# A chunked recurrence on one core: three loads with stacked keys, second copies of the decays by transfer, memory parts handed back one by one

## The chip, the cores and the metric

One core of a Trainium2 chip. The metric is the device time of one execution in microseconds, the median of several runs. Engines are TensorE (PE, its weight loads PEld), VectorE (DVE), ScalarE (ACT), GpSimd (POOL) and SyncE (SP, which here only issues transfers).

## What is computed

One decoder layer, float32, 2048 tokens by 1024 features: RWKV-7 time mixing, a layer norm, a gated MLP with a causal convolution, a layer norm. The change lies in the recurrence of the time mixing, 16 heads of 64:

```
def step(state, inp):
    r_t, w_t, k_t, v_t, kk_t, a_t = inp
    sa = jnp.einsum('bhij,bhj->bhi', state, -kk_t)
    state = (state * w_t[:, :, None, :]
             + sa[..., None] * (kk_t * a_t)[:, :, None, :]
             + v_t[..., None] * k_t[:, :, None, :])
    return state, jnp.einsum('bhij,bhj->bhi', state, r_t)
```

## The kernel before, in words

The work falls into four stages. `a_nodes` computes the projections r, k, v and the decay, and stores them to DRAM. `s_nodes` (L758) runs the recurrence. `w_nodes` (L1188) normalises, gates and multiplies by the output matrix. `f_nodes` (L1448) is the MLP. Products in the projections and the MLP are made of three passes over a high and a low part of each operand.

No order is written by hand. Every piece of work is a node of a planner (`Plan`, L59) with an engine, an estimated duration, a priority, dependencies, and slots that it takes and gives back. `order` (L81) simulates the engines with these durations, starts at each free engine the ready node of lowest priority number whose slots are free, and emits the instructions in that order. Each engine, and SP with its transfers, then runs its queue in order. So a duration in the planner changes only the order.

The recurrence is turned into matrix form over chunks of 64 rows. 2048 rows are 16 tiles of 128 rows, two chunks c each. A tile is prepared in two halves h of 512 columns (8 heads, or 4 pairs p of heads e = 0, 1):

- one load brings five inputs r, kp, kkn, b, th of a half into one single-buffered tile l (L846 to L848, slot lds);
- csI is the running sum of th, a product with a triangular matrix (L850);
- three exponentials make the decays P, Pe and Pi (L855 to L863);
- r is multiplied by P (L879), kkn by Pe (L875), and both are transposed (L902) into AR (L905);
- b and kp are multiplied by Pi into BKn (L922 to L930): eight products of 64 rows by 256 columns, since b and v, or k and state, swap their row halves between the two heads of a pair. The last of them gives the slot lds back;
- BKn is transposed (L932) and copied into BKT, one tile per head with the other head's rows zero (L939 to L943; the zeros are set once, L811);
- G = BKT x AR, four 128-row products per chunk and head (L948), masked into Gm (L954).

After both halves of a tile the 32x32 diagonal blocks are inverted on VectorE in 31 dependent steps of a multiply and an add (L984 to L998). The blocks go there through DRAM: NU is stored (L965), read back as NUs (L972), the start value XU is copied from a constant (L977); the result goes back by XD (L1000) and XT (L1010), and is completed by two small products per chunk (L1020 to L1053). Then the state is carried over the two chunks (L1076 to L1159): copy the state into UV (L1107), Z, copy, SA, copy into UV, dS, add, multiply by PC; Y is the output. The v rows of UV come from DRAM in four transfers of 256-byte pieces (L1067). From tile 12 on the eight pairs of a chunk go in two groups.

AR, BKn, Gm and PC exist four times each. The first product of a tile takes one of each (L844, L880), the last Y product gives all four back (L1156).

Of the kernel before, what the change touches and what calls it, by code (L numbers as in the profile page):

```python
# [11 lines left out]
F32 = mybir.dt.float32  # L12
# [3 lines left out]
OP = mybir.AluOpType  # L16
# [120 lines left out]
class K:  # L137
# [43 lines left out]
    def run(self, phases="ASWF", scratch=None):  # L181
        tc, nc, a = self.tc, self.nc, self.a
        with ExitStack() as ctx:
# [3 lines left out]
            for t in range(NT):  # L187
# [3 lines left out]
                for h in range(2):  # L191
# [3 lines left out]
                    for i, q in enumerate(("r", "kp", "kkn", "b", "th")):  # L195
                        self.S[q, t, h] = s[0:128, i] if q == "kkn" else s[1:129, i]
                    self.S["kk0", t, h] = s[128:129, 2]
# [33 lines left out]
    def a_nodes(self, ctx, pl):  # L231
# [56 lines left out]
        for sw, (q, wi, mm, ml) in enumerate((("k", 1, 2, 4), ("r", 0, 0, 1), ("v", 2, 3, 5))):  # L288
# [271 lines left out]
            for nq, (g, h, tl) in enumerate(order):  # L560
# [194 lines left out]
              slots=dict(lds=1, pw=4, P=1, Pi=1, Pe=1, AR=4, BKn=4, Gm=4, PC=4, BKT=1, NUs=2, XU=2, XT0=1, XT1=1, X11=2, mp=1,  # L755
                         FT=2, UV=2, c0=1, c1=1, Y=1, Yt=1))

    def s_nodes(self, ctx, pl, n_1, n_2, w, f):  # L758
# [12 lines left out]
        st_bkt = [0]  # L771
        eo = lambda tl: tl.rearrange("q (p e) i -> q p e i", e=2)
        ends, end1, xds, stores = [], [], [], []
        def f_open1():

            nonlocal inv, wkp, ldp, pw, xui, triI, gmask, cols, gm4, nbI, nbIn, nbE, scE
# [7 lines left out]
            ldp = E(name="s_ld", bufs=sl["lds"])  # L784
            pw = E(name="s_pw", bufs=sl["pw"], space=PSUM)
            xui = inv.tile([128, 512], F32, name="c_xui", bufs=1)
# [4 lines left out]

            for i in range(sl["BKT"]):
                BKTs.append([wkp.tile([128, 4, 128], F32, name=f"BKT{i}{e}") for e in range(2)])
# [26 lines left out]
        def f_c():  # L820
            for x, nm in ((triI, "c_triI"), (cols, "c_cols"), (gmask, "c_gmask"), (xui, "c_xui")):
                self.ld(x, a[nm])
        inv = wkp = ldp = pw = xui = triI = gmask = cols = gm4 = nbI = nbIn = nbE = scE = None
        cst = wk = ch2 = sm = pm = pc = None
        chs, XTs, BKTs, SV, ZS, SW, V = [None] * sl["AR"], [], [], {}, {}, {}, {}
        n_o1 = pl.add("-", 0, 0, f_open1, [n_1])
        n_o2 = pl.add("-", 0, 0, f_open2, [n_o1, n_2])
        n_z1 = pl.add("POOL", 2.0, -9.0, f_zero1, [n_o1], lat=0.2)
# [8 lines left out]
        for t in range(NT):  # L837
# [3 lines left out]
            grams, pcs, ars = [], [], {}  # L841
            for h in range(2):
                hb = b + h * o["hs"]
                first = ("AR", "BKn", "Gm", "PC") if h == 0 else ()  # L844

                def f_load(t=t, h=h):  # L846
                    self.ld(tile_of(t, f"l{h}", ldp, [128, 5, 512], tag="lds"), self.S["in", t, h])
                n_l = pl.add("SP", 0.5, -9.0 if t + h == 0 else hb + o["lds"], f_load, [n_o1], take=("lds",), lat=5.2)  # L848

                def f_cs(t=t, h=h, tri=None, nm=None):  # L850
                    ps = tile_of(t, (nm, h), pw, [128, 512], tag="pw")
                    MM(ps, tri, V[t][f"l{h}"][:, 4])
                n_ci = pl.add("PE", 0.86, hb, lambda f=f_cs: f(tri=triI, nm="csI"), [n_l] + [n_c] * (t == 0), take=("pw",))

                def f_exp(t=t, h=h, nm=None, src=None, bias=None, sc=None):  # L855
                    x = tile_of(t, (nm, h), wkp, [128, 512], tag=nm, bufs=sl[nm])
                    nc.scalar.activation(x, V[t][src, h], AF.Exp, bias=bias, scale=sc)
                n_P = pl.add("ACT", 0.57, hb + 0.2, lambda f=f_exp: f(nm="P", src="csI", bias=nbI, sc=-CDEC),
                             [n_ci], take=("P",))
                n_Pe = pl.add("ACT", 0.57, hb + 0.3, lambda f=f_exp: f(nm="Pe", src="csI", bias=nbE, sc=scE),  # L860
                              [n_ci, n_P], take=("Pe",))
                n_Pi = pl.add("ACT", 0.57, hb + 0.4, lambda f=f_exp: f(nm="Pi", src="csI", bias=nbIn, sc=CDEC),
                              [n_ci, n_Pe], take=("Pi",), give=("pw",))  # L863

                def f_alloc(t=t):
                    tile_of(t, "AR", chs[t % len(chs)], [128, 2, 8, 2, 64])
                    tile_of(t, "BKn", chs[t % len(chs)], [128, 2, 16, 64])
                    tile_of(t, "Gm", chs[t % len(chs)], [128, 2, 2, 8, 128])
                    tile_of(t, "PC", inv, [128, 8, 2], bufs=sl["PC"])

                def f_M(t=t, h=h, first=h == 0, f_alloc=f_alloc):
                    l = V[t][f"l{h}"]
                    if first:
                        f_alloc()
                    TT(l[:, 2], l[:, 2], V[t]["Pe", h], op=OP.mult)  # L875

                def f_R(t=t, h=h):
                    l = V[t][f"l{h}"]
                    TT(l[:, 0], l[:, 0], V[t]["P", h], op=OP.mult)  # L879
                n_M = pl.add("DVE", 0.6, hb + 0.5, f_M, [n_Pe] + [n_o2] * (t > 0 and h == 0), take=first, give=("Pe",))  # L880
                if h == 0:
                    n_alloc = n_M
                n_R = pl.add("DVE", 0.6, hb + 0.6, f_R, [n_P])

                def f_pcp(t=t, h=h):
                    pcp = tile_of(t, ("pcp", h), pw, [128, 4, 2, 64], tag="pw")
                    for p in range(4):
                        nc.tensor.transpose(pcp[:, p].rearrange("q c t -> q (c t)"),
                                            V[t]["P", h][:, p * 128:(p + 1) * 128], self.ident)
# [916 lines left out]
```

## Time and profile before

| | us |
|---|---|
| median of 3 runs (lowest to highest) | 2947.77 (2944.63 to 2948.37) |
| the profiled execution, its own time | 2945.05 |
| its span, first to last instruction | 2943.1 |
| busy in the span: TensorE / VectorE / ScalarE | 2803.2 / 2086.2 / 1742.4 |

A busy share is an average over four stages with different limits; the stages have to be looked at one by one. Matmuls overlap in their records, so the time of one record is longer than its share of the engine.

### The profile page before, as it was taken

Reading aid. Unit: us, or ns where it says so; the run is one execution under the profiler, and the core shown is the slowest. Engines: PE = TensorE matmul, PEld = TensorE weight load, DVE = VectorE, ACT = ScalarE, POOL = GpSimd, SP = SyncE. Lnnn points to the kernel's source line nnn. Section 1 sums busy time; section 2 is a strip of 40 time slices with the busy share of each in tenths; the row PEclk is TensorE's granted clock in tenths of the full one; section 3 lists DMA queues with packets and bytes.
Section 4 is the critical chain, followed back from the end, with each engine's and each line's share of the span. In section 5 each row is a group of like instructions: output and inputs, shape, how many; then the busy total and the mean of one; then the engine's idle time right before and its main releaser. Section 6 shows DMA issues by size and latency. Waiting matters only on the chain.

```text
span 2943.1 us, 51765 instructions
## 1 busy us (share of the span) xinstructions
PE 2803.2 (95%) x19392; PEld 2317.1 (79%) x19392; DVE 2086.2 (71%) x4288; ACT 1742.4 (59%) x4668; POOL 53.7 (2%) x96
## 2 busy tenths in 40 slices
PE   7998999998789999789999999999999999999997
PEld 5776778887677777678888888888888888888886
DVE  7888768986899999779865555475554745548454
ACT  8888657764578877887554444444444444444441
POOL 0000000001000000001100000000000000000000
PEclk9999999999899999899999999999999999999999
DMA  6446555435456656568652323343333432334222
GB/s 199 148 167 220 184 186 185 158 119 176 120 151 160 161 159 157 140 207 307 208 185 95 101 96 121 98 151 101 101 119 99 153 98 90 129 97 159 92 90 79
DMA packets 298555, 424.08 MB, mean 144 GB/s; under 512 B 153952, under 2 KB 179552, under 8 KB 294208
## 3 DMA queue, kind: packets, MB, share of 16 engines
q1 hardware_dynamic: 286976, 379.87, 41.3%
q0 software_dynamic: 11328, 40.90, 3.9%
q8 instruction: 153, 2.51, 0.4%
q14 instruction: 98, 0.80, 0.1%
HBM read 311.57 MB, written 109.12 MB: 143 GB/s over the span
## 4 chain that ended last, share of the span: by engine, by line
issue 55%; PE 21%; DVE 12%; ACT 7%; DMA 3%; POOL 1%; SPq 0%; POOLq 0%; ACTq 0%; DVEq 0%
PE ps L164 4%; PE ps L165 4%; PE ps L166 4%; DVE BKn L928 3%; ACT junk L643 2%; PE G L768 2%; DVE XU L995 2%; DVE itmp L990 2%; DVE Gm L955 1%; DMA l<-in 1%; PE Y L768 1%; DMA in<-av 1%; DVE l L879 1%; ACT junk L1283 1%; DVE l L875 1%
## 5 line engine op out<-in xcount | busy, mean ns | idle before, releaser
L166 PE MATMUL ps<-xH,wiL 128*128 128x512 f32 x1408 | 548.2, 389 | 0.5 <-DVE wiL L1594 0.5
L164 PE MATMUL ps<-xH,wiH 128*128 128x512 f32 x1408 | 548.1, 389 | 0.0
L165 PE MATMUL ps<-xL,wiH 128*128 128x512 f32 x1408 | 547.8, 389 | 0.0
L1594 DVE TENSOR_TENSOR wiL<-wis,wiH 128x1024 fp32r<-128x1024 f32 x176 | 215.4, 1224 | 459.0 <-ACT wiH L1455 459.0
L1455 ACT ACTIVATE hb<-ps 128x512 f32<-128x512 f32 x176 | 105.7, 601 | 484.4 <-PE ps L166 484.4
L164 PE MATMUL ps<-WH,xiH 128*128 128x512 f32 x768 | 305.1, 397 | 16.4 <-ACT xiH L255 9.5
L166 PEld LDWEIGHTS ps<-xH,wiL 128*128 128x128 f32 x1408 | 264.3, 188 | 56.9 <-DVE wiL L1594 2.1
L165 PEld LDWEIGHTS ps<-xL,wiH 128*128 128x128 f32 x1408 | 264.3, 188 | 54.8
L164 PEld LDWEIGHTS ps<-xH,wiH 128*128 128x128 f32 x1408 | 264.3, 188 | 54.6
L165 PE MATMUL ps<-WL,xiH 128*128 128x512 f32 x768 | 302.8, 394 | 2.2 <-DVE WL L350 2.2
L166 PE MATMUL ps<-WH,xiL 128*128 128x512 f32 x768 | 301.9, 393 | 0.0
L1622 DVE SCALAR_TENSOR_TENSOR cv<-hb,cw,cv 128x512 f32<-128x512 f32 x352 | 263.7, 749 | 19.9 <-ACT cv L1618 13.7
L165 PE MATMUL acc<-woL,aH 128*128 128x512 f32 x688 | 268.2, 390 | 2.2 <-DVE woL L1559 2.2
L164 PE MATMUL acc<-woH,aH 128*128 128x512 f32 x688 | 267.8, 389 | 0.0
L166 PE MATMUL acc<-woH,aL 128*128 128x512 f32 x688 | 267.7, 389 | 0.0
L1455 ACT ACTIVATE wiH<-wis 128x1024 fp32r<-128x1024 f32 x178 | 189.0, 1062 | 6.5 <-DMA wis<-in_w_in_dram 6.5
L164 PEld LDWEIGHTS ps<-WH,xiH 128*128 128x128 f32 x768 | 146.4, 191 | 54.6 <-ACT xiH L255 9.5
L1455 ACT ACTIVATE woH<-wos 128x512 fp32r<-128x512 f32 x172 | 108.7, 633 | 110.5 <-PE acc L166 103.9
L165 PEld LDWEIGHTS ps<-WL,xiH 128*128 128x128 f32 x768 | 146.3, 190 | 33.0 <-DVE WL L350 3.0
L166 PEld LDWEIGHTS ps<-WH,xiL 128*128 128x128 f32 x768 | 146.2, 190 | 31.2 <-DVE xiL L474 0.2
L165 PEld LDWEIGHTS acc<-woL,aH 128*128 128x128 f32 x688 | 129.1, 188 | 30.6 <-DVE woL L1559 4.0
L164 PEld LDWEIGHTS acc<-woH,aH 128*128 128x128 f32 x688 | 129.1, 188 | 27.4 <-ACT woH L1455 0.5
(243 smaller groups left out, 5349.3 us busy)
## 6 DMA issues: line engine op xcount, KB each, us to landing
wis<-in_w_in_dram SPq DMA_DIRECT2D x176, 512.0 KB
wos<-in_w_out_dram SPq DMA_DIRECT2D x172, 256.0 KB
l<-in SPq DMA_DIRECT2D x32, 1280.0 KB
xT<-in_xT_dram SPq DMA_DIRECT2D x21, 1028.0 KB
in<-kp SPq DMA_DIRECT2D x64, 256.0 KB
stg<-in_w_rkv_dram SPq DMA_DIRECT2D x48, 256.0 KB
gs<-gs SPq DMA_DIRECT2D x24, 512.0 KB
in<-kr SPq DMA_DIRECT2D x32, 256.0 KB
```

What stands on the lines that cost most here:

```text
L164: nc.tensor.matmul(ps, lH, rH, start=start, stop=False)
L165: nc.tensor.matmul(ps, lH, rL, start=False, stop=False)
L166: nc.tensor.matmul(ps, lL, rH, start=False, stop=stop)
L643: nc.scalar.activation(junk, Z["kr"][:, 64 * i:64 * i + 64], AF.Square, accum_out=st["ss"][:, tl, i:i + 1])
L768: MM = lambda out, l, r, **kw: nc.tensor.matmul(out, l, r, **{**dict(start=True, stop=True), **kw}, skip_group_check=True)
L875: TT(l[:, 2], l[:, 2], V[t]["Pe", h], op=OP.mult)
L928: TT(dst[rows, :, e], pe8(l[:, 1 if part else 3], e), pe8(V[t]["Pi", h], e), op=OP.mult)
L990: TT(V[t]["tv"], V[t]["XU"][:, 0:m, s:s + 1].to_broadcast([128, m, n]), V[t]["NUs"][:, s:s + 1, s + 1:32].to_broadcast([128, m, n]), op=OP ...
L995: TT(x, x, V[t]["tv"], op=OP.add)
L1455: CP = lambda out, in_, **kw: nc.scalar.activation(out, in_, AF.Copy, **kw)
L1594: TT(W["L"], W["s"], W["H"], op=OP.subtract)
L1622: STT(R[j], W["hb"][:, i:i + 512], C["cw"][:, fc, i:i + 1], R[j], op0=OP.mult, op1=OP.add)
```

## The change

The diff below is cut; "..." marks what is left out. In words:

- the five inputs are stored in the order r, kkn, b, kp, th and come in as three tiles with a slot each: th (lth), r and kkn (lrk), and b over kp stacked by chunk (lbk, two transfers): rows 0 to 63 of chunk c hold b, rows 64 to 127 hold kp, for all heads alike;
- P and Pe are two halves of one tile, and r and kkn are multiplied by them in one product of 128x1024;
- Pi is made by two exponentials of 64 rows, each on the rows of its chunk; two transfers inside SBUF then copy it to the other 64 rows, and one product of 128x1024 makes BKn;
- BKT is one 128-row tile with no zeros (two buffers), copied in one instruction; G uses rows 0 to 63 for head 0 and 64 to 127 for head 1, both heads in one node;
- all readers of the left blocks of Gm and of UV use rows 0 to 63 for both heads; the v rows of UV come in two transfers of whole rows; XU is loaded by SP and not copied by ScalarE;
- AR, Gm, BKn and PC are each taken where first written and given back where last read;
- many planner durations are changed, in the recurrence, the output projection and the MLP.

```
-                    for i, q in enumerate(("r", "kp", "kkn", "b", "th")):
+                    for i, q in enumerate(("r", "kkn", "b", "kp", "th")):
...
-              slots=dict(lds=1, pw=4, P=1, Pi=1, Pe=1, AR=4, BKn=4, Gm=4, PC=4, BKT=1, ...
+              slots=dict(cs=1, lth=1, lrk=1, lbk=1, pw=4, P=1, Pi=1, AR=4, BKn=4, Gm=4, PC=4, BKT=2, ...
...
-        def f_zero1():
-            for x in BKTs:
-                for e in range(2):
-                    nc.gpsimd.memset(x[e], 0.0)
...
-                n_l = pl.add("SP", 0.5, -9.0 if t + h == 0 else hb + o["lds"], f_load, [n_o1], take=("lds",), lat=5.2)
+                def f_lt(t=t, h=h):
+                    self.ld(tile_of(t, ("th", h), ldp, [128, 512], tag="lth"), self.S["in", t, h][:, 4])
+                def f_lr(t=t, h=h):
+                    self.ld(tile_of(t, ("rk", h), ldp, [128, 2, 512], tag="lrk"), self.S["in", t, h][:, 0:2])
+                def f_lb(t=t, h=h):
+                    x = tile_of(t, ("bk", h), ldp, [128, 2, 512], tag="lbk")
+                    for part in range(2):
+                        self.ld(x[es(part)], self.S["in", t, h][:, 2 + part].rearrange("(c t) i -> t c i", c=2))
+                lb = -9.0 if t + h == 0 else hb + o["lds"]
+                n_lt = pl.add("SP", 1.0, lb - 0.3, f_lt, [n_o1], take=("lth",), lat=2.5)
+                n_lr = pl.add("SP", 1.9, lb, f_lr, [n_o1], take=("lrk",), lat=2.7)
+                n_lb = pl.add("SP", 1.9, lb + 0.3, f_lb, [n_o1], take=("lbk",), lat=2.7)
...
+                def f_Pi(t=t, h=h):
+                    x = tile_of(t, ("Pi", h), wkp, [128, 2, 512], tag="Pi", bufs=sl["Pi"])
+                    for c in range(2):
+                        nc.scalar.activation(x[es(c), c], V[t]["csI", h][es(c)], AF.Exp, bias=nbIn[es(c)], scale=CDEC)
+                def f_Px(t=t, h=h):
+                    for c in range(2):
+                        self.ld(V[t]["Pi", h][es(1 - c), c], V[t]["Pi", h][es(c), c])
+                n_P = pl.add("ACT", 1.24, hb + 0.2, f_P, [n_ci], take=("P",))
+                n_Pi = pl.add("ACT", 1.4, hb + 0.4, f_Pi, [n_ci, n_P], take=("Pi",), give=("cs", "pw"))
+                n_Pi = pl.add("SP", 0.6, hb + 0.5, f_Px, [n_Pi], lat=2.5)
+                def f_MR(t=t, h=h):
+                    TT(V[t]["rk", h], V[t]["rk", h], V[t]["P", h], op=OP.mult)
+                n_MR = pl.add("DVE", 1.13, hb + 0.5, f_MR, [n_P, n_lr])
...
+                    n_t = pl.add("PE", 0.5, hb + 0.9 + 0.3 * i, f_tr, [n_MR] + trs, take=("pw",), give=("lrk",) if i else ())
...
-                                TT(dst[rows, :, e], pe8(l[:, 1 if part else 3], e), pe8(V[t]["Pi", h], e), op=OP.mult)
+                    TT(V[t]["BKn"][:, :, 8 * h:8 * h + 8].rearrange("q c h i -> q c (h i)"), V[t]["bk", h], V[t]["Pi", h],
+                       op=OP.mult)
+                n_bk = n_bks[h] = pl.add("DVE", 1.13, hb + 1.1, f_bk, [n_Pi, n_lb] + ([n_bks[0]] if h else aw),
+                                         take=() if h else ("BKn",), give=("Pi", "lbk"))
...
-                            CP(x[e][es(e)], V[t]["tb", h, c][es(e)])
+                        CP(tile_of(t, ("BKT", h, c), wkp, [128, 4, 128], tag="BKT", bufs=sl["BKT"]), V[t]["tb", h, c])
+                    def f_g(t=t, h=h, c=c):
+                        G = [tile_of(t, ("G", h, c, e), pw, [128, 4, 128], tag="pw") for e in range(2)]
+                        for p in range(4):
+                            for e in range(2):
+                                MM(G[e][:, p], V[t]["BKT", h, c][es(e), p],
+                                   V[t]["AR"][es(e), c, 4 * h + p].rearrange("q a t -> q (a t)"))
+                    n_g = pl.add("PE", 1.09, hb + 2.2 + c, f_g, [n_bt] + evs, take=("pw", "pw"), give=("BKT",))
...
-                CP(x.rearrange("q m t -> q (m t)"), xui)
+                self.ld(x.rearrange("q m t -> q (m t)"), a["c_xui"])
-            n_xu = pl.add("ACT", 0.52, ib, f_xu, [n_nu], take=("XU",))
+            n_xu = pl.add("SP", 1.0, ib - 12, f_xu, [n_o1], take=("XU",), lat=2.5)
...
-                            MM(mp[r + 32:r + 64, p], V[t]["Gm"][r:r + 32, e, c, p, 32:64], V[t]["X11", c][r:r + 32, p],
-                               tile_position=(r, r + 32))
+                            MM(mp[r + 32:r + 64, p], V[t]["Gm"][0:32, e, c, p, 32:64], V[t]["X11", c][:, e, p],
+                               tile_position=(0, r + 32))
...
-                    for e in range(2):
-                        self.ld(eo(UV[:, c])[es(1 - e), :, e], src[:, :, e])
+                    self.ld(UV[64:128, c].rearrange("t h i -> t (h i)"), self.S["vc", t][64 * c:64 * c + 64])
...
+                n_y1 = pl.add("PE", 1.08, sb + 4, f_y1, prevS + evs + ars[0] + [n_z2] + (n_ga if c else []), take=("Y",),
+                              give=("AR",) if c else ())
...
+                    n_ds = pl.add("PE", 1.08 * d, sp, f_ds, n_su[-1:], give=("BKn",) if c and lastu else ())
...
-                              give=("AR", "BKn", "Gm", "PC", "UV") if c else ())
+                              give=("Gm", "UV") if c else ())
...
-                    n_mm = pl.add("PE", 5.14, pr, f_mm, [n_w] + xn, take=("w_" + e,), give=("f_wi",))
+                    n_mm = pl.add("PE", 5.47, pr, f_mm, [n_w] + xn, take=("w_" + e,), give=("f_wi",))
```

## Rows read from the trace of the kernel before

**Rows 1.** Busy time in windows: start:end, length, PE, PEld, DVE, ACT, POOL, PEclk, DMA share, GB/s.

```profile
960.00:1020.00 60.00, 55.31 (x1067) 47.07 (x1065) 57.70 (x185) 48.02 (x96) 1.07 (x2) 1.00 0.62 157
...
1500.00:1560.00 60.00, 60.00 (x269) 49.67 (x268) 41.99 (x50) 33.22 (x67) 0.86 (x1) 1.00 0.51 176
```

**Rows 2.** The same columns, cut at starts of half tiles.

```profile
719.20:783.85 64.65, 45.70 (x377) 37.24 (x377) 50.92 (x155) 28.37 (x59) 1.66 (x4) 0.79 0.53 140
...
932.35:1059.20 126.85, 116.52 (x2226) 99.54 (x2225) 121.88 (x393) 102.47 (x204) 2.13 (x4) 1.00 0.62 160
...
1188.95:1282.00 93.05, 70.31 (x1535) 61.87 (x1534) 69.57 (x210) 76.71 (x222) 4.85 (x9) 0.85 0.57 148
```

**Rows 3.** The chain of waits, 690 to 1300 us: start, length, what.

```profile
719.19 1.14 PE csI L768 x2
...
725.69 8.73 DMA l<-in
...
1162.37 9.64 DMA l<-in
...
1188.95 0.86 PE csI L768 x2
```

**Rows 4.** Groups by line and shape, 932.35 to 1059.20: count, busy us, mean ns.

```profile
L768 PE MATMUL G<-AR,BKT 128*128 128x128 f32 x257 | 35.5, 283 | 0.0
...
L928 DVE TENSOR_TENSOR BKn<-l,Pi 64x256 f32<-64x256 f32 x64 | 26.5, 419 | 1.1
...
L767 ACT ACTIVATE BKT<-tb 64x512 f32<-64x512 f32 x32 | 19.0, 592 | 4.9 <-PE tb L936 4.3
...
L1024 DVE STREAM_TRANSPOSE X<-XT 64x256 f32<-64x256 f32 x16 | 7.0, 436 | 0.3
...
L768 PE MATMUL mp<-X,Gm 32*32 32x32 f32 x256 | 5.5, 192 | 0.0
...
L857 ACT ACTIVATE Pi<-csI,c_cols 128x512 f32<-128x512 f32 x8 | 5.5, 693 | 0.0
...
L879 DVE TENSOR_TENSOR l<-l,P 128x512 f32<-128x512 f32 x8 | 5.5, 684 | 0.0
...
L767 ACT ACTIVATE Zs<-Z 128x512 f32<-128x512 f32 x8 | 4.8, 597 | 0.1
...
L767 ACT ACTIVATE XU<-c_xui 128x512 f32<-128x512 f32 x4 | 2.5, 630 | 0.1
```

**Rows 5.** Groups by line, the whole span.

```profile
L1315 DVE TENSOR_TENSOR yg<-yg,gs 128x1024 f32<-128x1024 f32 x24 | 29.1, 1218 | 0.0
```

**Rows 6.** Timeline of SP's transfer issues, 960 to 996 us: start, length, issue, count.

```profile
963.39 1.26 SPq L147 DMA_DIRECT2D XD<-XU  x2
967.04 4.67 SPq L147 DMA_DIRECT2D XT<-XD  x8
972.04 0.34 SPq L147 DMA_DIRECT2D l<-in  x1
974.80 2.61 SPq L147 DMA_DIRECT2D UV<-vc  x4
979.85 2.58 SPq L147 DMA_DIRECT2D NU<-Gm  x4
985.13 1.11 SPq L147 DMA_DIRECT2D NUs<-NU  x2
988.66 0.34 SPq L147 DMA_DIRECT2D l<-in  x1
```

**Rows 7.** Timeline of VectorE, 960 to 1000 us.

```profile
987.74 0.86 DVE L928 TENSOR_TENSOR BKn<-l,Pi 64x256 f32<-64x256 f32 x2
```

**Rows 8.** Timeline of TensorE, 960 to 1000 us.

```profile
976.36 1.15 PE L768 MATMUL Y<-state,AR 64*64 64x64 f32 x32
...
977.44 1.16 PE L768 MATMUL G<-AR,BKT 128*128 128x128 f32 x8
...
980.15 1.02 PE L768 MATMUL csI<-l,c_triI 128*128 128x512 f32 x2
```

More of the change, by code (lines that the diff above doesn't have):

```diff
@@ L840, in s_nodes @@
             P = lambda off, b=b: b + off
-            grams, pcs, ars = [], [], {}
+            grams, pcs, ars, n_bks = [], [], {}, {}
             for h in range(2):
                 hb = b + h * o["hs"]
-                first = ("AR", "BKn", "Gm", "PC") if h == 0 else ()
-                def f_load(t=t, h=h):
-                    self.ld(tile_of(t, f"l{h}", ldp, [128, 5, 512], tag="lds"), self.S["in", t, h])
-                n_l = pl.add("SP", 0.5, -9.0 if t + h == 0 else hb + o["lds"], f_load, [n_o1], take=("lds",), lat=5.2)
[L850 to L883, printed above, removed]
@@ new lines, in s_nodes, with f_cs @@
+                lb = -9.0 if t + h == 0 else hb + o["lds"]
+                n_lt = pl.add("SP", 1.0, lb - 0.3, f_lt, [n_o1], take=("lth",), lat=2.5)
+                n_lr = pl.add("SP", 1.9, lb, f_lr, [n_o1], take=("lrk",), lat=2.7)
+                n_lb = pl.add("SP", 1.9, lb + 0.3, f_lb, [n_o1], take=("lbk",), lat=2.7)
+                def f_cs(t=t, h=h):
+                    MM(tile_of(t, ("csI", h), pw, [128, 512], tag="pw"), triI, V[t]["th", h])
+                n_ci = pl.add("PE", 1.06, hb, f_cs, [n_lt] + [n_c] * (t == 0), take=("cs", "pw"), give=("lth",))
@@ L939, in f_bt @@
                     def f_bt(t=t, h=h, c=c):
-                        x = V[t]["BKT", h, c] = BKTs[st_bkt[0] % len(BKTs)]
-                        st_bkt[0] += 1
-                        for e in range(2):
-                            CP(x[e][es(e)], V[t]["tb", h, c][es(e)])
-                    n_tb = pl.add("PE", 0.44, hb + 2.0 + c, f_tb, n_bks[2 * c:2 * c + 2], take=("pw",))
-                    n_bt = pl.add("ACT", 0.96, hb + 2.1 + c, f_bt, [n_tb, n_z1], take=("BKT",), give=("pw",))
-                    gs = []
@@ new lines, in s_nodes @@
+                    n_tb = pl.add("PE", 0.47, hb + 2.0 + c, f_tb, [n_bk], take=("pw",))
+                    n_bt = pl.add("ACT", 0.49, hb + 2.1 + c, f_bt, [n_tb], take=("BKT",), give=("pw",))
+                    def f_g(t=t, h=h, c=c):
[4 more added lines that the diff above has]
+                                   V[t]["AR"][es(e), c, 4 * h + p].rearrange("q a t -> q (a t)"))
@@ L958, in s_nodes @@
-                        gs.append(n_g)
-                        grams.append(pl.add("DVE", 0.6, hb + 2.3 + c + 0.1 * e, f_gm, [n_g], give=("pw",)))
+                        grams.append(pl.add("DVE", 0.6, hb + 2.3 + c + 0.1 * e, f_gm, [n_g] + (grams[:1] or aw),
+                                            take=() if h + c + e else ("Gm",), give=("pw",)))
             e0 = (t == 0) * o["e0"]
@@ new lines, in s_nodes @@
+                    n_w.append(pl.add("DVE", 0.6 if nh == 1 else 0.33, sp, f_w, [n_ds, *prevS] + n_w[-1:], give=bk))
+                    n_s1.append(pl.add("DVE", 0.6 if nh == 1 else 0.33, sp, f_s1, n_w[-1:] + n_s1[-1:] + [prevY] + pcs,
+                                       give=("PC",) if c and lastu else ()))
+                n_y2 = pl.add("PE", 1.08, sb + 4.5, f_y2, n_su + [n_y1] + (n_s1 if c else []),
+                              give=("Gm", "UV") if c else ())
+                n_yt = pl.add("ACT", 1.22, sb + 5, f_yt, [n_y2], take=() if c else ("Yt",), give=("Y",))
@@ L1396, in w_nodes @@
                 else:
[L1397 removed]
+                    n = pl.add("PE", 5.46, pr + 5.2 * h, lambda t=t, h=h, e=e: [f_mm(t, h, k, e) for k in range(KD)],
                                yn[t] + list(wn.values()) + [n_late], take=("w_pz" + e,), give=("w_y",) if h else ())
@@ L1566, in wout @@
                 if 0 < f < NF - 1:
-                    accs[h] = [pl.add("PE", 2.56, pr, lambda: [acc_mm(f, h, tl, R["H"], R["L"]) for tl in range(4)],
+                    accs[h] = [pl.add("PE", 2.73, pr, lambda: [acc_mm(f, h, tl, R["H"], R["L"]) for tl in range(4)],
                                       [nw, an[f]] + before, give=("f_ao",) + ("f_a",) * h)]
@@ L1735, in f_nodes @@
             for tl in range(4):
-                n = pl.add("PE", 3.84, pr, lambda tl=tl: [m(tl) for m in mm], nw + [an[f] for f in range(NF)] + [n])
+                n = pl.add("PE", 4.12, pr, lambda tl=tl: [m(tl) for m in mm], nw + [an[f] for f in range(NF)] + [n])
                 pr += 3.84
```

139 lines of the change are left out of this document (66 added, 73 removed).

## The prediction

> **What bounds the kernel now.** I read the stretches of the span first, to find where an engine is not full. Before about 700 us the input projections run, from about 1300 us on the output projection and the MLP. In 1500 to 1560 TensorE is busy 60.00 of 60 us, so a change to the recurrence can gain nothing there. Between them lies the recurrence (L758 to L1168): in 960 to 1020 VectorE is busy 57.70 us, TensorE 55.31, ScalarE 48.02 [rows 1]. The second table cuts at the starts of half tiles. A half tile is 512 columns of a 128-row tile, 32 in all, and each begins with one csI product. In 932.35 to 1059.20, which is four tiles or eight halves, a half takes 126.85/8 = 15.86 us, of which VectorE is busy 121.88/8 = 15.24 (96.1%), TensorE 14.57 (91.9%), ScalarE 12.81 (80.8%) [rows 2].
>
> Then the chain of waits, for what sets the pace of the halves. The third csI starts at 719.19, the 32nd at 1188.95: 29 halves in 469.76 us, 16.20 each. In that chain stand waits for the load of a half's five inputs, 8.73 and 9.64 us [rows 3]. The timelines of one half show why: the load is issued at 972.04, the csI that reads it starts at 980.15, the last BKn products run 987.74 to 988.60, and the next load is issued at 988.66 [rows 6, 7, 8]. The input buffer is single and is given back by the last BKn product only, so load (8.1 us) and work (8.5 us) alternate: a ring of 16.6 us. Two limits of the same size thus stand side by side, a full VectorE and a ring through one buffer, and relieving one alone would gain little. The change touches both.
>
> **The change, part by part.** Per half, from the sums over eight halves.
>
> VectorE. The eight BKn products of 64x256 go, 26.5/8 = 3.31 us; so do the products with P and with Pe (that row is like the P row), 2 x 5.5/8 = 1.38 [rows 4]. In come two products of 128x1024, one of inputs 0 and 1 with P, one of inputs 2 and 3 with Pi. A 128x1024 product takes 1.22 us [rows 5]: 2.44. Net -2.25, VectorE 12.99 per half. The X11 transposes shrink from 64 to 32 partitions at the same 256 columns. No row shows one; the bounds are half of its 7.0/8 = 0.88 us per half less or more; I take nothing, the middle.
>
> ScalarE. Four BKT copies of 64x512 become two of 128x512: 19.0/8 = 2.38 becomes 2 x 0.597 = 1.19 (the Zs row). The XU copy (0.63 per tile) becomes a load, -0.32. P and Pe stay two exponentials. Pi becomes two of 64x512, each no longer than the present one of 0.69, so at most +0.69 [rows 4]. Net -0.8 or better: 12.0.
>
> TensorE. G keeps its count, but the zero-padded 128-row products become pairs on rows 0 to 63 and 64 to 127. Bounds: nothing saved, or half of 35.5/8 = 4.44, that is 2.22 [rows 4]. I take half: 32 products of 64 columns on disjoint halves take 1.15 us (Y<-state,AR), 8 of 128 columns 1.16 (G) [rows 8]; half the columns explain a factor of two of these four, running side by side the other. Then 12.35 per half; unpaired, 14.57. The first merge product now reads rows 0 to 31 for both heads; if its pairs ran one after the other, its 5.5/8 = 0.69 would double, and 13.0 would still not be above VectorE. That SA, Z, dS and Y read re-ordered rows costs nothing: their shapes stay. A rule supports the half: "TensorE: Matmul & The Clock Gate" (Part 3: Packing small matmuls) of the Trainium skill says that products on different row groups run at the same time. By it the sum stands; without it, the second rival's.
>
> Loads and SP. The load becomes th, r with kkn, and b with kp (two issues), each buffer given back on its own: th after csI, r/kkn after the transposes, b/kp after the BKn product. Each single-buffer ring is now a part of the 8.1 us landing plus one or two operations, at most 8.1 + 2 x 1.22 + about 1, so under 12 us. One new link appears: Pi's second copy, two transfers of 128 KB inside SBUF, issued on SP behind the exponentials. No row shows such a transfer. Below, XD stores of 128 KB: issued 963.39 to 964.65, the loads that wait for them issue from 967.04, so 2.4 us or less; above, the 9.64 us of a whole half [rows 6, 3]. I take 3, being nearest in size to XD. Pi's ring is then exponentials 1.4, issue 1.2, landing 3, product 1.22, hand-offs about 1: 8 us, hidden inside a half; with the upper bound about 14.5, not hidden. SP's issues per tile go from 22 to 31: UV -2, the loads +6, the copies +4, XU +1. UV's four took 2.61 us, eight XT 4.67 [rows 6], so about 0.6 each: +5.4 us of SP per tile, beside 12.9 now (the seven rows [rows 6]), against a tile of 28. What is queued behind a copy that waits for ScalarE are the NU, XD and XT transfers of other tiles, which are due about three tiles later; XU's load goes out 12 us ahead of its use. Cost zero while a tile has that slack.
>
> Memory parts given back separately. Tile 15's first csI starts about 1172.05 (where the 9.64 us load ended) [rows 3] and the stretch to its last output ends at 1282.00 [rows 2]: some 110 us, with four copies 27.5 us per tile or 13.7 per half. That would be the next limit. AR, BKn and PC now return before the last Y product, which lowers it by a few us. I count no gain, but it is a reason not to expect the full share of VectorE below.
>
> Planner costs. They re-order nothing before the recurrence. In the MLP TensorE is full [rows 1], which covers small shifts on the other engines; priced at zero, bounds 3 us either way. The two memsets of the zero halves go from GpSimd: nothing waits on them in the steady state.
>
> **Sum.** VectorE needs 12.99 us per half. At today's 96.1% a half takes 13.52; but TensorE at 12.35 and ScalarE at 12.0 then stand at 91% and 89%, and three nearly full engines wait on each other more. I take for the fullest engine the share that the second-fullest reaches today, 91.9%: 14.13. Times 29 halves, 409.9 instead of 469.8: -59.9 us. Before the third half and in the tail of 93 us after the 32nd (VectorE 69.57 busy [rows 2], waits along one tile's chain) I take nothing. The profiled execution, 2945.05 us (span 2943.1 and 1.95 around it), becomes 2885. The median of the runs is 2.7 above that execution, so **2888 us**.
>
> **The rivals.**
> - *All three engines stay packed.* The share stays 96.1%: 29 x 13.52 = 392, -78; the first 65 us, where VectorE is busy only 50.92 because of the load ring [rows 2], may add 5. About 2865. For it: today's share; against: TensorE and ScalarE have less air.
> - *G does not pair.* TensorE keeps 14.57 and becomes the bound: at 96.1%, 15.16 per half, -30 us, 2918. For it: no row has two products on disjoint row halves without also splitting columns.
> - *Nothing moves.* The recurrence's own chain of eight hand-offs per 64-row step, or the order that the planner writes for costs that differ from the real ones, holds a half near 16. About 2943. Against: VectorE is full today, so the chain has never been the shown limit.
> - *The copy of Pi becomes the ring (slower).* It waits on SP behind other waits, then in the transfer queues behind the bulk loads of the next half: SP held by one XT group 4.67, exponentials 1.4, landing 9.64, product 1.22 and hand-offs 1 give 17.9 us per half, +1.7 x 29 = +50, 2998. It decides once copy and wait together exceed about 13 us. For it: the landings in rows 3; against: the bulk loads of the next half are freed mostly after the copy has gone out. "DMA: Bandwidth & Descriptors" (Queues, rings and completion order) of the Trainium skill speaks for it: each transfer engine takes a queue's descriptors in ring order. It gives the copy no way past a load already issued.
>
> **How the numbers follow.** Forecast (a half between 13.8 and 14.8 us) 0.56, packed engines 0.13, unpaired G 0.16, nothing moves 0.07, copy ring 0.08. The forecast's own span of halves gives 2878 to 2907. The range goes from the packed case with 10 us from the first stretch, 2860, to the unpaired case with the same half at 15.6 instead of 15.16, 2930; it leaves out the last two cases and a little below. A measurement here can tell 0.2% (5.9 us) from no change. Faster: the first three and a third of the fourth, 0.87; same: 0.05; slower: 0.08.
>
> **What would show it.** Right: halves 14.1 us apart, the BKn and P products at 1.2 us once each, no wait of csI for a load, VectorE above 90%. Wrong: G still at 1.1 us per 8 products; BKn products waiting for the Pi transfer; a half still above 15.5 with VectorE below 85%, which would mean an order or chain limit. Gains outside 690 to 1290 would contradict the whole argument.

## The result: no gain, a small loss

The changed kernel takes 2965.6 us (median, 2960.5 to 2972.1) against 2946.8 in the runs beside it (2944.6 to 2948.4): ratio 1.0057, 95% interval 1.0046 to 1.0069. The forecast was 2888 us with a range of 2860 to 2930. The kernel came out **slower**, so neither forecast nor range holds. The profiled execution after spans 2963.5 us, 20.4 more than that of before.

**The work shrank as predicted.** The windows of the changed kernel, with the columns and stretches of [rows 1, 2], and one longer stretch:

```profile
932.35:1059.20 126.85, 107.58 (x2200) 88.93 (x2196) 105.83 (x313) 96.81 (x194) 2.12 (x4) 0.96 0.79 189
840.00:1140.00 300.00, 256.42 (x5177) 216.00 (x5172) 251.05 (x776) 221.06 (x443) 5.32 (x10) 0.91 0.75 181
960.00:1020.00 60.00, 54.21 (x1149) 45.71 (x1148) 51.45 (x141) 49.30 (x102) 1.06 (x2) 0.97 0.79 190
1500.00:1560.00 60.00, 60.00 (x270) 49.68 (x269) 42.31 (x50) 34.87 (x68) 0.86 (x1) 1.00 0.54 186
```

The longer stretch in the kernel before:

```profile
840.00:1140.00 300.00, 273.81 (x5184) 234.02 (x5186) 286.96 (x915) 239.02 (x478) 5.34 (x10) 0.99 0.62 161
```

In 960 to 1020 VectorE fell from 57.70 us busy to 51.45, and the transfers' share rose from 0.62 to 0.79. The groups by line and shape, 840 to 1140, show the operations of [rows 4, 5] at their forecast prices: each stacked product 1.22 us, once a half.

```profile
L768 PE MATMUL G<-AR,BKT 64*128 64x128 f32 x576 | 44.9, 293 | 2.5 <-ACT Pi L863 2.1 <-ACT BKT L767 0.2
...
L933 DVE TENSOR_TENSOR BKn<-bk,Pi 128x1024 f32<-128x1024 f32 x19 | 23.2, 1223 | 10.3 <-DMA Pi<-Pi 6.5 <-DMA bk<-in 2.6 <-ACT UV L767 1.0
L874 DVE TENSOR_TENSOR rk<-rk,P 128x1024 f32<-128x1024 f32 x19 | 23.2, 1221 | 8.8 <-DMA rk<-in 8.7 <-issue 0.2
L1029 DVE STREAM_TRANSPOSE X<-XT 32x256 f32<-32x256 f32 x38 | 16.3, 429 | 1.6 <-DMA XT<-XD 1.1
```

**The pace did not move.** I measure it between the last output products (Y from UV and Gm) of tile 0 and tile 13. In TensorE's timeline of before they stand at

```profile
802.58 1.15 PE L768 MATMUL Y<-UV,Gm 128*64 128x64 f32 x32
...
1219.32 1.10 PE L768 MATMUL Y<-UV,Gm 128*64 128x64 f32 x32
```

and after at

```profile
806.06 1.10 PE L768 MATMUL Y<-UV,Gm 128*64 128x64 f32 x32
...
1216.66 1.98 PE L768 MATMUL Y<-UV,Gm 128*64 128x64 f32 x32
```

So a tile takes 416.7/13 = 32.1 us before and 410.6/13 = 31.6 after. Two profiles whose written order is the same through tile 13 read 31.1 and 31.7 (e2_pi_act and e4_both below differ in durations of later stages only); b1_wf_new, with the order of the kernel before, reads 32.4, and e1_wf_old, with that of the changed one, 32.0. So a pace is known to about 0.6 us, and before and after are alike.

The prediction counted from the third csI to the 32nd. After the change these stand at

```profile
715.93 1.02 PE L768 MATMUL csI<-th,c_triI 128*128 128x512 f32 x2
...
1169.50 1.13 PE L768 MATMUL csI<-th,c_triI 128*128 128x512 f32 x2
```

That is 453.6 us for 29 halves, 15.64 each: 16 us less than the 469.8 of before, where 60 less were forecast. The starts of halves can run ahead of the outputs (in e2_pi_act below they come 14.7 apart while the outputs keep their pace), so I go by the outputs.

At 31.6 us a tile, VectorE works 251.05/300 x 31.6/2 = 13.2 us a half (forecast 12.99), ScalarE 11.6 (12.0), TensorE 13.5 (12.35, at a mean granted clock of 0.91 in place of 0.99). What VectorE saved, it now waits. Before, this view of 840 to 1140 has a single line, 1.2 us for Gm; after, its longest are (what waited, for what: us in all, times, longest):

```profile
DVE itmp L995 <- DMA NUs<-NU: 9.8, 4, 3.8
DVE rk L874 <- DMA rk<-in: 8.7, 5, 3.8
DVE Gm L962 <- PE G L768: 7.0, 6, 2.6
DVE BKn L933 <- DMA Pi<-Pi: 6.5, 8, 2.3
DVE BKn L933 <- DMA bk<-in: 2.6, 1, 2.6
```

**Where the 20 us are.** First and last starts by tile name, changed kernel:

```profile
L768 PE MATMUL csI<-th,c_triI x64: 590/595/1220, 691.0 to 1170.0; 128*128 128x512 f32 x64
...
L767 ACT ACTIVATE Yt<-Y x64: 573/592/597, 797.9 to 1265.2; 64x512 f32<-64x512 f32 x64
...
L164 PE MATMUL z<-woH,yE x28: 388/389/796, 1277.5 to 1308.5; 128*128 128x512 f32 x28
...
L1460 ACT ACTIVATE hb<-ps x176: 581/601/602, 1495.8 to 2880.5; 128x512 f32<-128x512 f32 x176
```

and before:

```profile
L768 PE MATMUL csI<-l,c_triI x64: 590/594/1061, 682.7 to 1189.2; 128*128 128x512 f32 x64
...
L767 ACT ACTIVATE Yt<-Y x64: 583/592/596, 790.5 to 1281.7; 64x512 f32<-64x512 f32 x64
...
L164 PE MATMUL z<-woH,yE x28: 389/389/504, 1275.4 to 1314.2; 128*128 128x512 f32 x28
...
L1455 ACT ACTIVATE hb<-ps x176: 579/601/605, 1489.3 to 2860.0; 128x512 f32<-128x512 f32 x176
```

| us, profiled execution | before | after | after later by |
|---|---|---|---|
| first csI | 682.7 | 691.0 | 8.3 |
| tile 0, last output product | 802.6 | 806.1 | 3.5 |
| tile 13, last output product | 1219.3 | 1216.7 | -2.6 |
| last Yt (end of the recurrence) | 1281.7 | 1265.2 | -16.5 |
| first product of the output projection (z) | 1275.4 | 1277.5 | 2.1 |
| first hb of the MLP | 1489.3 | 1495.8 | 6.5 |
| last hb | 2860.0 | 2880.5 | 20.5 |

The recurrence's end came 16.5 us forward, nearly all of it in its last two tiles, the output projection began 2.1 us later all the same, and the MLP grew from 1370.7 to 1384.7 us.

### The profile page after: what moved, and what is told of

It is laid out like the page before. It is cut to its first block, busy times and chain, and to the rows that moved or that the text cites. A ratio compares the mean times of both kernels' runs of the same rounds, so it can differ in the third digit from the quotient of the medians.

```text
span 2963.5 us, 51632 instructions
## 1 busy us (share of the span) xinstructions
PE 2783.4 (94%) x19392; PEld 2289.4 (77%) x19392; DVE 2019.1 (68%) x4032; ACT 1717.9 (58%) x4620; POOL 52.9 (2%) x94
## 4 chain that ended last, share of the span: by engine, by line
issue 55%; PE 20%; ACT 8%; DVE 7%; DMA 7%; POOL 1%; SPq 1%; POOLq 0%; DVEq 0%; ACTq 0%
PE ps L164 4%; PE ps L165 4%; PE ps L166 4%; ACT junk L643 3%; DMA Pi<-Pi 1%; DVE itmp L995 1%; DVE XU L1000 1%; PE Y L768 1%; ACT UV L767 1%; DMA bk<-in 1%; DVE Gm L962 1%; PE mp L768 1%; DMA in<-av 1%; PE Z L768 1%; DMA NUs<-NU 1%
## 5 line engine op out<-in xcount | busy, mean ns | idle before, releaser
L165 PE MATMUL acc<-woL,aH 128*128 128x512 f32 x688 | 270.1, 393 | 11.6 <-DVE woL L1564 11.6
```

The lines of the kernel that those rows point to most:

```text
L165: nc.tensor.matmul(ps, lH, rL, start=False, stop=False)
```

## The experiments

Time differences below are differences of ratios to the kernel before, times 2947 us; the interval of one is some 4 to 10 us either way.

### The MLP: is it the planner's durations?

```diff
# e1_wf_old: after; b1_wf_new: before, the other way round; eleven lines such as
-  n_mm = pl.add("PE", 5.47, pr, f_mm, ...)
+  n_mm = pl.add("PE", 5.14, pr, f_mm, ...)
-  cn.append(pl.add("DVE", 1.45, pr + 5, f_s, [n], ...))
+  cn.append(pl.add("DVE", 1.2, pr + 5, f_s, [n], ...))
```

> The changed kernel with the eleven durations that the planner holds for the output projection and the MLP set back to those of before. Theory A (the new durations put a product that waits for a load ahead of the weight's low part in VectorE's queue at the three block joins, and TensorE stands 3 to 4 us and then runs at the low clock): the 14 us that the MLP lost come back, 2951 us, and the three 60-us windows 1980, 2340 and 2700 show TensorE busy for 60 again. Theory B (the joins lose because everything arrives later after the recurrence): no change, 2965 us within 3. Under A part of the 18.6 us that are lost between the end of the recurrence and the start of the MLP may come back as well (2935 to 2951).

> The kernel before with those eleven new durations and nothing else. Theory A (durations alone re-order VectorE at the joins): slower by about 14 us, 2961 us, with the loss at the three joins. Theory B (the joins lose because of the recurrence): 2947 us within 3.

Measured: e1_wf_old 1.0011 (0.9999 to 1.0022), 13.6 us faster than the changed kernel; b1_wf_new 1.0065 (1.0046 to 1.0084), 19 us slower than before by durations alone. The MLP (first to last hb) takes 1370.3 us in the first, 1385.8 in the second. VectorE's timeline of the changed kernel at the first block join shows the mechanism:

```profile
1983.91 1.23 DVE L1658 TENSOR_TENSOR xr<-xr,ag 128x1024 f32<-128x1024 f32 x1 [1.93 <-DMA xr<-xn]
1985.06 1.22 DVE L1659 TENSOR_TENSOR xr<-xr,ab 128x1024 f32<-128x1024 f32 x1
1986.19 0.68 DVE L1564 TENSOR_TENSOR woL<-wos,woH 128x512 fp32r<-128x512 f32 x1
```

and TensorE's the price:

```profile
1982.67 0.39 PE L164 MATMUL acc<-woH,aH 128*128 128x512 f32 x1
1986.93 0.79 PE L165 MATMUL acc<-woL,aH 128*128 128x512 f32 x1 [3.87 <-DVE woL L1564]
1987.52 0.63 PE L166 MATMUL acc<-woH,aL 128*128 128x512 f32 x1
...
1992.63 0.39 PE L166 MATMUL ps<-xH,wiL 128*128 128x512 f32 x1
```

The low part woL of a weight stands in VectorE's queue behind a product that waits for a load; TensorE stands 3.87 us for it and then runs at the lower of its two clock levels (granted 0.50, 1.2 GHz, in 1987 to 1992) for 5 us more: 0.63 us a product in place of 0.39. At the second and third join it stands 3.34 and 2.64 us. The three pauses, 9.9 us, and the slow products behind the first (2.6) and the third (1.7) make up the 14 us. In e1_wf_old the same window is full again:

```profile
1980.00:2040.00 60.00, 60.00 (x266) 49.38 (x265) 42.04 (x49) 24.49 (x48) 1.07 (x2) 1.00 0.50 168
```

where the changed kernel has

```profile
1980.00:2040.00 60.00, 56.13 (x236) 45.90 (x235) 35.76 (x42) 22.04 (x43) 0.53 (x1) 0.94 0.39 133
```

Theory A holds, by both experiments. The change carries an edit of durations that costs 14 us and has nothing to do with the recurrence.

### The copy of Pi: is it the slow rival?

```diff
# e2_pi_act: both copies of Pi by ScalarE, four exponentials
-  nc.scalar.activation(x[es(c), c], csI[es(c)], ...)
+  for d in range(2):
+      nc.scalar.activation(x[es(d), c], csI[es(c)], ...)
# e3_pi_actq: the transfer issued on ScalarE's queue
-  self.ld(Pi[es(1 - c), c], Pi[es(c), c])
+  self.st2(Pi[es(1 - c), c], Pi[es(c), c])
-  n_Pi = pl.add("SP", 0.6, hb + 0.5, f_Px, [n_Pi], lat=2.5)
+  n_Pi = pl.add("ACT", 0.2, hb + 0.41, f_Px, [n_Pi], lat=3.5)
```

> The changed kernel with the second copy of the inverse decays made by two more ScalarE exponentials of 0.68 us, in place of two transfers on SP's queue. Theory P (the copy's wait on SP and its landing pace a half: 3.7 us from issue to product, plus up to 4 us of SP's queue): a half goes from 15.8 towards 14.5 us, 29 halves give 38 us, some of which the output projection gives back: 2930 to 2950 us, recurrence ends 25 to 40 us earlier. Theory O (the order that the planner writes, with memory parts as the limit, paces it): within 5 us of 2965, and the idle time of VectorE's product moves to its load or to another releaser. ScalarE rises by 1.4 us a half, from about 44 to 49 of 60, too little to bind.

> The changed kernel with the second copy still transferred, but issued from ScalarE's queue right behind the exponentials, not from SP's queue. If SP's in-order queue is what delays the copy (it stood up to 4 us behind a transfer that waited for the inverse): 10 to 30 us faster, 2935 to 2955. If the landing itself (about 2 us) or the order is what counts: within 5 us of 2965, or some us slower as ScalarE is held for the issue.

Measured: e2_pi_act 1.0048 (1.0032 to 1.0065), 3 us faster, not told apart from the changed kernel; e3_pi_actq 1.0092 (1.0062 to 1.0123), 10 us slower, at the edge of the interval of that difference. Theory P falls: the pace in e2_pi_act is 31.1. The copy's wait is gone, and VectorE waits elsewhere (840 to 1140):

```profile
DVE itmp L992 <- DMA NUs<-NU: 21.4, 9, 3.4
DVE Gm L959 <- PE G L768: 10.8, 11, 3.6
DVE BKn L930 <- DMA bk<-in: 1.8, 2, 1.4
```

The two findings add up in a version that is level with the kernel before:

> The changed kernel with the second decay copy made by ScalarE and with the old durations for output projection and MLP together. In the profiles the first brought the end of the recurrence 12.6 us and the MLP's start 8.8 us forward, the second gave the MLP 14 us back. If they add: 2943 to 2951 us, level with the kernel before. If the old durations re-order the recurrence's tail (the profile of that run alone had its recurrence 9 us later): 2955 or more.

Measured: 0.9991 (0.9982 to 1.0001). Against e1_wf_old, from which it differs by the copy alone, that is 6 us less, a little more than the interval of some 4.5: the copy may cost a few us, not the 50 of the rival.

### The four memory parts: do they pace it?

```diff
# e5_bkn3 (after)       BKn=4 -> BKn=3
# b2_gm3 (before)       Gm=4 -> Gm=3
# e12_joint (after): all four taken at a tile's first product (r and kkn), given back after the last Y
-  n_MR = pl.add("DVE", 1.13, hb + 0.5, f_MR, [n_P, n_lr])
+  n_MR = pl.add("DVE", 1.13, hb + 0.5, f_MR, ..., take=() if h else ("AR", "BKn", "Gm", "PC"))
```

> The changed kernel with three memory parts for the stacked keys (BKn) in place of four, so that a tile's key product waits for the last state update of the tile three before it, not four. Theory R (the ring of four parts paces the recurrence: in the changed kernel the product of tile t+4 starts 2 to 15 us, median 5, after the state product of tile t that frees its part, and lifetime 121 plus wait 5 make 4 times 31.6): the pace per tile rises from 31.6 us to at least 35 (105 over 3) and up to 42 (126 over 3), so that the end comes 45 us or more later, 3010 us and above. Rival V (VectorE or TensorE with their queues pace it, and the parts are seldom the reason): within 10 us of 2965.

> The kernel before with three sets of a tile's memory parts in place of four (there all four kinds are taken together, so one kind limits all). Theory R for both kernels (121 us lifetime per tile and 8.5 us from the release to the next product make 4 times 31.7 there too): pace 35 to 42 us a tile, 45 to 140 us slower, 2990 to 3090. Rival V (VectorE at 96 percent sets the pace before, and the parts have slack): under 15 us slower, 2947 to 2962.

> The changed kernel with the four memory parts of a tile taken together at the first key product and given back together after the last output product, as before the change. If taking them separately is worth something (the front may run up to 10 us further into a tile whose parts are not all free): 5 to 25 us slower than the changed kernel, 2970 to 2990. If the early front only fills the queues and lengthens the tile's chain (140 us from cumulative sum to last output against 121 before): as fast or faster, 2950 to 2968.

Measured: e5_bkn3 1.0189 (1.0161 to 1.0217), 39 us slower than after, pace 33.8; b2_gm3 1.0425 (1.0404 to 1.0446), 125 us slower, pace 40. In the kernel before a tile's lifetime hardly shrinks when only three fit (118 us, and 40 x 3 = 120). In the changed kernel it shrinks from 123 to 102 (from the first key product to the last dS, median of tiles 2 to 12): its tiles live longer than they must, because the front runs ahead. Its result lies between the two forecasts. e12_joint is at 1.0117 (1.0097 to 1.0137), 18 us slower: **taking the parts separately is worth 18 us**, the one clear gain of the change.

### A tile's chain through memory

```diff
# e10_cut (after): the inversion's load reads a constant, without waiting for the store
-  self.ld(x[es(e)], self.NU[t].rearrange(...))      # n_ns after n_nu
+  self.ld(x[es(e)], a["c_xui"].rearrange(...))       # n_ns after n_o1
# e7_nus (on e4_both): the planner is told longer landings
-  f_nus, [n_nu], take=("NUs",), lat=3.0     +  lat=6.0   (rk 2.7 -> 4.5, bk 2.7 -> 4.0)
# e13_xuact (on e4_both): XU copied by ScalarE, not loaded
-  self.ld(x, a["c_xui"])                     +  CP(x, xui)
```

> The changed kernel with the inversions fed from a constant of the same size and not from the products' corner that was just stored (the store stays, the load no longer waits for it): a part of the computation is left out, each inverse is that of a constant. This cuts the store, the load and VectorE's stand of 17.5 us in 350 out of every tile's chain; VectorE's, ScalarE's and TensorE's work is the same. Theory C (the pace is a tile's chain through two round trips to memory, divided by four parts): the pace falls from 31.6 us a tile to 29 or less and the end comes 40 us or more earlier, a start 20 us earlier included. Rival W (VectorE's in-order queue finds another wait in its place): the pace stays above 30.5 and only the earlier start is left, 20 us or less.

> The kernel e4_both with the planner told longer landings: 6.0 us in place of 3.0 for the loads that start an inversion, 4.5 for 2.7 for the receptances, 4.0 for 2.7 for the keys, so that VectorE's order puts other work ahead of what waits for them. Theory L (in-order VectorE stands 22 us in 350 before the first step of an inversion and 5 before the receptance product, and that paces the recurrence): 15 to 27 us faster than e4_both, 2920 to 2930. Rival Q (these stands are slack, the pace lies with the tile's chain): within 6 us of 2946.

> The kernel e4_both with the identity for an inversion copied by ScalarE from a constant again, not loaded for every tile (256 KB and one issue less a tile, 0.5 us of ScalarE more). If the transfers' load (DMA engines busy 0.72 against 0.60 before) stretches the landings that VectorE waits for: 5 to 15 us faster than e4_both, 2931 to 2941. If not: within 3 us of 2946.

Measured: e10_cut leaves the true inverse out, so its time serves the argument only. It is at 0.9985 (0.9974 to 0.9995), 21 us faster; its first output stands 32 us earlier (773.8 against 806.1, tile 0), but its pace is 32.2, as rival W says. From the release of a key part to the product that takes it again pass 9.9 to 29 us in ten of twelve tiles (2 to 15, median 5, in the changed kernel). With that much air in the ring of parts the pace is the same, so the ring does not pace the changed kernel either. VectorE's waits in e10_cut show what came instead:

```profile
DVE BKn L933 <- DMA Pi<-Pi: 18.8, 7, 5.0
DVE Gm L962 <- PE G L768: 10.2, 11, 1.7
DVE itmp L995 <- DMA XU<-in_c_xui_dram: 6.4, 3, 4.1
```

e7_nus is at 1.0011 (0.9999 to 1.0024), 6 us slower than e4_both, with the wait for NUs down to 2.7 and others in its place:

```profile
DVE Gm L959 <- PE G L768: 16.6, 13, 3.4
DVE stmp L1142 <- PE dS L768: 11.0, 9, 3.5
...
DVE itmp L992 <- DMA NUs<-NU: 2.7, 2, 1.8
```

e13_xuact, 0.9985 (0.9975 to 0.9995), is 2 us from e4_both, not told apart; the transfers' share is 0.66 against 0.67 there, so this edit took little away (the Pi copy's end had taken it from 0.75 to 0.67). The waits for Pi and for NUs were taken away in turn, and VectorE's busy time in 300 us stayed between 240 and 253: something else is always missing when it is free.

### What does added work cost?

```diff
# b3_dve (before), e8_dve (after): two of four masked products of a half made twice
+  for _ in range(2 - e):
       TT(Gm[:, e, c, 4 * h:4 * h + 4], G[h, c, e], gm4, op=OP.mult)
# e9_pe (after): csI made twice;  e16_act (after): both exponentials of P made twice
```

> The kernel before with two of the four masked products of a half made twice (the same values again, 0.69 us each, so 1.2 to 1.37 us more VectorE in every half, 32 halves, the planner's durations as they were). Theory V (VectorE, 96 percent busy, sets the half of before): 29 halves lengthen by all of it, 35 to 40 us, 2982 to 2988. Theory R (the round of the four memory parts sets it): VectorE's work counts only where it lies on a tile's own chain, under half of it, 5 to 18 us.

> The changed kernel with the same doubling, 1.2 to 1.37 us more VectorE in every half. If VectorE still sets the half: 35 to 40 us, 3000 to 3006. If what paces it lies elsewhere (VectorE is idle 10 of 60 us): under 15 us, below 2980.

> The changed kernel with the cumulative-sum product made twice in every half (the same values, about 1.06 us more TensorE a half, 34 us over 32 halves). If TensorE, 81 to 85 percent busy at a mean clock of 0.93, sets the half: 25 to 35 us, 2990 to 3000. If not: under 10 us; the added work could even raise the clock a little.

> The changed kernel with the two exponentials of the decays made twice in every half (the same values, 0.69 and 0.77 us, so 1.25 to 1.46 us more ScalarE a half, 40 to 47 us over 32 halves). VectorE's addition counted with about 0.6 of its time, TensorE's with a quarter. If ScalarE, 74 percent busy, is the hidden limit: 35 us or more, 3000 and above. If the three engines' in-order queues share the path: 8 to 25 us, 2974 to 2991. If ScalarE has slack: under 6 us.

| added | work added, us | slower by, us | share that counts |
|---|---|---|---|
| VectorE, before | 38 to 44 | 34 | about 0.8 |
| VectorE, after | 38 to 44 | 22 | about 0.5 |
| TensorE, after | 28 to 34 | 6 | 0.2 |
| ScalarE, after | 40 to 47 | 6 | 0.1 |

With an interval of some 6 or 7 us, the last two are not told apart from no cost at all. VectorE did set the kernel before. In b3_dve it stays full and the tiles stretch to 34.7 us:

```profile
840.00:1140.00 300.00, 259.30 (x4762) 217.98 (x4759) 286.73 (x872) 219.74 (x436) 4.80 (x9) 0.97 0.55 145
```

After the change VectorE's queue still counts most, though it is idle 16% of the time: in e8_dve its busy time rises, and half of what is added fits into the waits.

```profile
840.00:1140.00 300.00, 251.41 (x4966) 208.49 (x4962) 262.32 (x788) 213.28 (x425) 4.79 (x9) 0.91 0.72 172
```

### Order and tail

```diff
# e6_xu_late (on e4_both): n_xu for tile 0 due 8 us later
# e11_uv (on e4_both):     uv=47.5 -> uv=56.0
# e15_hf16 (on e11_uv):    hf=12 -> hf=16
```

> The kernel e4_both with one edit: the first tile's identity load (XU), which in the changed kernel stands at the head of SP's queue and waits until 677.6 us for a TensorE product that still reads the memory, is put behind the first decay, key and constant loads. Theory S (the recurrence of the changed kernel starts 8 us late, first cumulative sum 691.0 against 682.7, because of this wait): the first cumulative sum moves to 683 to 686 and the end 3 to 8 us forward against e4_both. Rival: the first decay load waits for the same memory, then no change within 2 us.

> The kernel e4_both with the loads of v due 8.5 us later in a tile, so that they stand behind the stores and loads of the inverse in SP's queue and not before them. If SP's order delays the round trips (its queue is 77 percent full by the planner's durations): 5 to 16 us faster, 2930 to 2941. If not: within 3 us of 2946.

> The kernel e11_uv (second decay copy by ScalarE, old durations for output projection and MLP, loads of v due later) with the state updates of the last four tiles no longer cut into two halves, for fewer and wider instructions in the tail where ScalarE is 95 percent busy. If the tail is ScalarE's: 2 to 8 us faster than e11_uv, 2932 to 2938. If the serial chain of state updates sets the tail, which the cut shortens: 3 to 10 us slower, 2943 to 2950.

Measured: e6_xu_late 0.9997 (0.9986 to 1.0008), first csI at 690.8: no change. The first load did go out 7.3 us earlier, so the rival's reason (that it waits for the same memory) does not hold either:

```profile
677.99 0.38 SPq L147 DMA_DIRECT2D th<-in  x1
...
670.68 0.38 SPq L147 DMA_DIRECT2D th<-in  x1
```

(the changed kernel, then e6_xu_late). TensorE's timeline of the changed kernel shows what holds csI:

```profile
690.79 0.39 PE L166 MATMUL ps<-WH,xiL 128*128 128x512 f32 x1
691.02 1.02 PE L768 MATMUL csI<-th,c_triI 128*128 128x512 f32 x2
```

TensorE has no gap in the 25 us ahead of it, and in its written order csI stands behind 29 groups of 28 projection products, in the kernel before behind 28. One group takes 6.4 us, most of the 8.3.

e11_uv is at 0.9967 (0.9955 to 0.9979), 7 us faster than e4_both with the same operations, only due in another order. e15_hf16 **0.9936 (0.9922 to 0.9950), 2925.7 us**: 9 us faster than e11_uv, more than expected, and some 19 faster than the kernel before. Its tile rows:

```profile
L164 PE MATMUL z<-woH,yE x28: 388/397/497, 1247.9 to 1287.5; 128*128 128x512 f32 x28
...
L1457 ACT ACTIVATE hb<-ps x176: 579/601/603, 1463.1 to 2832.6; 128x512 f32<-128x512 f32 x176
```

In e11_uv the first z stands at 1271.2, 23.3 us later, but not all of that is the tail. Both kernels have the same order through tile 11, and tile 11's last output product already stands at 1157.4 in e11_uv's profile and at 1146.9 in this one: so far apart can two profiles of one order be. From there to the first z it takes 1271.2 - 1157.4 = 113.8 us and 1247.9 - 1146.9 = 101.0, so the tail gives 12.8.

## Why the prediction was wrong, step by step

- **The work per half** (VectorE -2.25, ScalarE -0.8, G side by side) was right: 13.2 and 11.6 us, and 16 G products in the time of 8. For the latter the prediction cited a rule: products on different row groups running at the same time (the Trainium skill, "TensorE: Matmul & The Clock Gate", Part 3). The trace agrees: 576 of them are busy 44.9 us, 78 ns each, against 35.5/257 = 138 [rows 4].
- **The step that failed in the recurrence** is "I take for the fullest engine the share that the second-fullest reaches today, 91.9%". Measured are 83.7% in 840 to 1140 (83.4% in the stretch that the prediction's shares came from), and 13.2/0.837 is 15.8, about the old half of 15.86. That is the prediction's own sign of being wrong, a half above 15.5 with VectorE below 85%, read by it as an order or chain limit. A share of busy time was carried from a kernel in which one engine had always work ready to one in which none has. In its place the runs show in-order queues that wait for each other: each wait that was taken away came back at another instruction, added VectorE work counts half, and other due times for one load moved 7 us (e11_uv). The rival "nothing moves" named this and got 0.07; its counter-argument (VectorE is full, so the chain was never the limit) says only what the limit was before.
- **"Gains outside 690 to 1290 would contradict"**: the loss outside did. "Priced at zero, bounds 3 us either way" for the planner's costs is the second step that failed: 14 us here, 19 alone. That TensorE was full told that it had no air, not that a new order would keep it fed.
- **The tail.** I took nothing there, but did not see that a gain ahead of it would be lost in it. From tile 13's last output product to the first z it takes 56.1 us before and 60.8 after (57 to 63 in e1_wf_old, e2_pi_act, e3_pi_actq, e4_both, e10_cut and e13_xuact, with that product anywhere from 1191.9 to 1225.0; 69 and 70 in e5_bkn3 and e12_joint). The first tiles of the output projection live in tile 13's parts (f_ch1 waits for that product), and their preparation stands in the same queues as the last state updates. SP's issues after show it, one gap of 30 us in which the next weight waits for its staging buffer:

```profile
1236.85 4.81 SPq L147 DMA_DIRECT2D XT<-XD  x8
1271.60 0.35 SPq L147 DMA_DIRECT2D wos<-in_w_o_dram  x1
```

 That buffer is given back by woL on VectorE, whose queue stands at state updates and then does the normalisation of finished tiles:

```profile
1260.19 0.42 DVE L1145 TENSOR_TENSOR stmp<-dS,state 128x256 f32<-128x256 f32 x1 [6.68 <-PE dS L768]
...
1270.85 0.69 DVE L1262 TENSOR_TENSOR woL<-wos,woH 128x512 fp32r<-128x512 f32 x1
```

 So the recurrence's end, 16.5 us earlier, was of no use.
- **The slower rival** had the right sign and the wrong cause. Without the transfer of Pi the time is only 3 to 6 us shorter. Its landing, taken as 3 us, is 2.8 to 6.3 in the eight places where it stands in the chain of waits (690 to 1300). The rule quoted with it (the Trainium skill, "DMA: Bandwidth & Descriptors", Queues, rings and completion order: a queue's descriptors are taken in ring order) would let the copy gain on a queue without loads. In e3_pi_actq, on ScalarE's queue, VectorE's wait for Pi does fall, from 6.5 us to 0.6 in 840 to 1140; but its wait for r and kkn rises from 8.7 to 20.3, and the time by 10 us. So here the copy's place in SP's order is not the price.
- **Memory parts, "I count no gain"**: they give 18 us (e12_joint). The start, taken as unchanged, came 8.3 us later; that is TensorE's written order and not a load, as e6_xu_late shows.

Not settled: which part of the change uses up what VectorE saved. Not the Pi copy beyond a few us, not XU's load, not the parts, not one engine's added time. Left are the stacked product, which makes both chunks of a half wait for one load and one copy; the loads through three single buffers; and the planner's durations in the recurrence itself, which the change rewrites too (a copy into UV from 1.04 to 1.3 us, an output product from 1.27 to 1.08) while its due times stay those of the kernel before. None of these was undone by itself; that moving two settings of the order gained 7 and 9 us (e11_uv, e15_hf16) speaks for the last. TensorE's lower clock is a further candidate: its work a half is 13.5 us in place of 12.35. By the share of added TensorE work that counts (0.2), 29 x 1.15 = 33 us would be worth some 7, an estimate that no run shows.

## What to carry to other kernels

Take work from the fullest engine and the next wait in its queue appears; before counting a gain, add a little work to each engine and see what share of it counts, and look at what is ready when the engine is free. Where a planner writes the order, an edit of its durations is a change of its own: time it alone. And a stage that ends earlier is worth only what the next stage's first instruction can use.

## What the runs showed of the hardware that was not expected

- A pause of TensorE can cost more than itself: after 3.87 us without work the granted clock was 0.50 and the products took 0.63 us in place of 0.39 until 1992.6, about 13 of them at 0.43 us spacing in place of 0.23, some 2.6 us more. It need not: after the 3.34 us of the second join the clock stayed at 1.00, and after the 2.64 us of the third it fell again (0.57 in 2716 to 2720).

```profile
2352.61 0.50 PE L165 MATMUL acc<-woL,aH 128*128 128x512 f32 x1 [3.34 <-DVE woL L1564]
2352.95 0.39 PE L166 MATMUL acc<-woH,aL 128*128 128x512 f32 x1
```

- With the change TensorE's mean granted clock fell from 0.99 to 0.91 in 840 to 1140, and some 30 us of added TensorE work (e9_pe) left it at 0.91.
- An exponential over 64 partitions takes as long as one over 128: 671 to 721 ns against 693 [rows 4].
